# Layer 0 of a two-layer hybrid backbone: ten input-projection blocks by seven products of halves ahead of the attention, staggered mLSTM heads, half of the output projection beside them

## The chip, the core and the metric

The kernel runs on one core of a Trainium2 chip. A core has five engines with queues of their own: TensorE multiplies matrices (PE in the profile; PEld is its loading of weights), VectorE (DVE) works element by element, ScalarE (ACT) applies functions and copies, GpSimd (POOL) does small arithmetic and starts transfers, and SyncE (SP) starts transfers. Matmuls write to PSUM, eight banks of 128 x 512 float32; everything else lives in SBUF. The metric is the device time of one execution in microseconds. Three runs of the kernel before took 3549.83, 3545.3 and 3549.78 us; the median is 3549.78.

## What is computed

1024 latent tokens and 256 context tokens of width 1024 pass through two layers. Each layer normalizes, scales and shifts its input, projects it, mixes over tokens, and projects back with a gated residual. Layer 0 has two mixers side by side, one projection in and one out:

```python
qa, ka, va, za, qb, kb, vb, ob, zb, g = _split_cols(h @ w_in, AB_SIZES)   # nine blocks of 1024 columns, 16 gate columns
...
if rotary:
    qb, kb = _axial_rope(qb), _axial_rope(kb)
...
oa_l = _neighbourhood_attention(qa_l, ka_l, va_l, ka_c, va_c, rpb)        # 16 heads of 64
hb_l, hb_c = _mlstm_bidir(mb_l, mb_c, need_ctx)                           # 4 heads of 256, both directions
...
hb = jnp.swapaxes(hb, 1, 2).astype(ob.dtype) * jax.nn.sigmoid(_heads(ob, ML_HEADS))
hb = _rms(hb, h_norm.reshape(ML_HEADS, ML_DIM))
ya = oa.reshape(oa.shape[:2] + (NA_WIDTH,)) * jax.nn.silu(za)
yb = hb.reshape(hb.shape[:2] + (ML_WIDTH,)) * jax.nn.silu(zb)
return jnp.concatenate([ya, yb], axis=-1) @ w_out
```

Layer 1 has 16 recurrent heads (HGRN2) in the same frame. The change concerns layer 0; layer 1's code is touched where it shares helpers.

## The kernel before

All large projections are float32 in three matmuls: each operand is split into a rounded high part and a low rest (`split`, L71 on ScalarE, L72 on VectorE), and `dense` (L120 to L122) adds high x high, high x low and low x high over 8 depth tiles of 128. The normalized input h of a layer lies transposed in SBUF as `hh` and `hl`, ten tiles of 128 tokens wide. Weights come from memory in slabs of 128 x 512 (`wraw`), are split, and wait in a ring of six slabs (`wring`).

A *block* is 256 columns of the projection for all ten token tiles: 10 x 8 x 3 = 240 matmuls of 256 columns. `proj_out` makes one: it evicts pairs of tiles into `ev` (two buffers) and stores them with a POOL DMA (L275). There are 24 such blocks: four of attention values (`na_values`) and q, k, v, o, z of the four mLSTM heads (`ml_ahead`), stored in `md`.

Layer 0 runs in this order: modulation and norm; gates and the modulation rows of both layers, with blocks 0 to 2 of the attention values beside them; the attention, eight pairs of heads (`na_attn`) of ten tiles each, with the next pair's q, k (`na_qk`), z (`na_z`) and one block beside each; the mLSTM; the output projection. The last twelve blocks stand under `filler`, which gives them a late priority, so that the scheduler of the language places them in gaps of the mLSTM.

The mLSTM takes the heads one after another. `ml_load` fetches all ten chunks of a head, rotates q and k on VectorE (`rope`, L413 to L416), transposes them on TensorE and makes the scores; `ml_rec` then walks ten chunks in both directions. A chunk in one direction (a *unit* below) is five float32 matmuls of 258 columns: L451 into `acc`, two of L461 with the state `mC`, two of L470 whose result L478 adds to the state. `ml_out` gates and normalizes a finished chunk (L507 to L513, with an inverse root on POOL, L147) and transposes it (L517) for `yd`.

The output projection has two column halves (b = 1, 0) and two depth halves: q = 0 is the attention's part of `yd`, q = 1 the mLSTM's. `out_ahead` makes q = 0 of b = 1 into `oacc`, then `out_tile` q = 1 of it and, from a second weight array of 16 slabs, all of b = 0, with the next layer's norm and transposes (`mod_tr`) beside the last.

Layer 1's v and z projections use seven products of halves already (`q_sums`, `q_seven`): tokens, depth and columns are halved, and seven products of sums of the halves take the place of eight. `q_form` adds and splits weights, L872 to L874 multiply, `q_out` combines.

The order on each engine is not written by hand: the scheduler sets it from priorities, the buffers of each pool and its own estimate of time. DMA queues and engines work through their own lists in order.

## Time and profile before

| | |
|---|---|
| median of three runs | 3549.78 us |
| the profiled execution | 3547.46 us |
| its span, first to last instruction | 3545.7 us |
| mean granted clock of TensorE | 0.992 |
| PE busy, share of span, instructions | 3473.2 us, 98%, x24618 |
| DVE busy | 2311.4 us, 65%, x6182 |
| ACT busy | 1550.8 us, 44%, x3587 |
| POOL busy | 538.4 us, 15%, x880 |
| DMA | 347.19 MB, mean 98 GB/s |

A row of a group reads: line, engine, operation, output tile <- input tiles, sizes, count | busy time in us, mean of one in ns | idle time of the engine just before, and what ended it. Float32 matmuls appear as two passes each. Matmuls are pipelined: the duration of one is longer than the distance to the next, so a busy TensorE is not the same as one at its peak.

### The profile page before, as it was taken

To read this page: it belongs to the slowest core of one execution; us is meant where nothing else is said; L and a number is where in the kernel's file an instruction comes from. 1 tells how busy PE (TensorE), PEld (TensorE's weight loads), DVE (VectorE), ACT (ScalarE), POOL (GpSimd) and SP (SyncE) were. 2 spreads that over 40 slices of the span, in tenths; PEclk is the share of its full clock that TensorE was granted. 3 is DMA by queue.
4 is the path that set the end of the run, shared out by engine and by line. 5 is a ranking of instruction groups with operands and counts; after the bars stand their busy time and mean duration, and the time that the engine had idled before them with its cause. 6 is when DMAs were issued, how large, how long until landed. Compare 5 with 4: busy or idle time off the path is not lost.

```text
span 3545.7 us, 65436 instructions
## 1 busy us (share of the span) xinstructions
PE 3473.2 (98%) x24618; PEld 3175.5 (90%) x24618; DVE 2311.4 (65%) x6182; ACT 1550.8 (44%) x3587; POOL 538.4 (15%) x880
## 2 busy tenths in 40 slices
PE   8999999999999999998989999999999999999999
PEld 5879999999999999997778999989999999999877
DVE  4646666666754756655556866577777777777853
ACT  5545555455533433333345333344444444444431
POOL 2222222222211212211101222000100000000010
PEclk9999999999999999999999999999999999999999
DMA  5532323222234334324653322211211211211354
GB/s 210 173 105 74 83 70 83 75 82 83 76 99 153 109 106 144 101 89 137 199 160 125 102 102 102 81 37 55 64 44 54 60 55 48 60 60 46 111 174 126
DMA packets 361964, 347.19 MB, mean 98 GB/s; under 512 B 31064, under 2 KB 314904, under 8 KB 361520
## 3 DMA queue, kind: packets, MB, share of 16 engines
q1 hardware_dynamic: 323472, 242.61, 23.5%
q0 software_dynamic: 38176, 100.40, 8.2%
q8 instruction: 194, 3.18, 0.4%
q14 instruction: 122, 1.00, 0.1%
HBM read 266.66 MB, written 76.08 MB: 97 GB/s over the span
## 4 chain that ended last, share of the span: by engine, by line
PE 83%; issue 8%; DMA 4%; DVE 2%; POOL 1%; ACT 1%; SPq 0%; POOLq 0%; ACTq 0%; DVEq 0%
PE mm L122 14%; PE mm L120 14%; PE mm L121 14%; PE s L1041 6%; PE acc L677 2%; PE tr L657 2%; PE mm L731 2%; PE mm L732 2%; PE mm L733 2%; PE sa L873 2%; PE sa L872 2%; PE sa L874 2%; PE s L470 1%; PE acc L461 1%; PE s L1086 1%
## 5 line engine op out<-in xcount | busy, mean ns | idle before, releaser
L122 PE MATMUL mm<-wh,hl 128*128 128x256 f32 x2560 | 749.5, 293 | 0.3 <-DVE hl L253 0.3
L120 PE MATMUL mm<-wh,hh 128*128 128x256 f32 x2560 | 747.1, 292 | 0.0
L121 PE MATMUL mm<-wl,hh 128*128 128x256 f32 x2560 | 746.0, 291 | 0.0
L122 PEld LDWEIGHTS mm<-wh,hl 128*128 128x128 f32 x2560 | 489.1, 191 | 11.1 <-issue 4.1
L120 PEld LDWEIGHTS mm<-wh,hh 128*128 128x128 f32 x2560 | 489.3, 191 | 7.7 <-issue 1.5
L121 PEld LDWEIGHTS mm<-wl,hh 128*128 128x128 f32 x2560 | 489.3, 191 | 7.1 <-issue 0.5
L122 PE MATMUL mm<-hh,wl 128*128 128x512 f32 (+1 forms) x1344 | 490.9, 365 | 0.0
L120 PE MATMUL mm<-hh,wh 128*128 128x512 f32 (+1 forms) x1344 | 485.0, 361 | 0.0
L121 PE MATMUL mm<-hl,wh 128*128 128x512 f32 (+1 forms) x1344 | 483.7, 360 | 0.0
L121 PEld LDWEIGHTS mm<-hl,wh 128*128 128x128 f32 x1344 | 254.0, 189 | 32.1
L122 PEld LDWEIGHTS mm<-hh,wl 128*128 128x128 f32 x1344 | 253.9, 189 | 30.3
L120 PEld LDWEIGHTS mm<-hh,wh 128*128 128x128 f32 x1344 | 254.3, 189 | 29.2
L71 ACT CAST wh<-wraw 128x512 fp32r<-128x512 f32 x274 | 168.7, 620 | 209.1 <-PE mm L121 126.3
L1032 ACT COPY gksel<-gK 128x512 f32<-128x512 f32 x224 | 146.9, 662 | 213.7 <-PE s L1041 204.6
L731 PE MATMUL mm<-woh,yh 128*128 128x512 f32 x524 | 210.6, 403 | 16.3 <-issue 10.1
L72 DVE TENSOR_TENSOR wl<-wraw,wh 128x512 fp32r<-128x512 f32 x274 | 185.1, 685 | 56.6 <-ACT wh L71 54.5
L733 PE MATMUL mm<-woh,yl 128*128 128x512 f32 x524 | 209.5, 400 | 0.0
L732 PE MATMUL mm<-wol,yh 128*128 128x512 f32 x524 | 208.8, 399 | 0.0
L1041 PE MATMUL s<-gQ,gksel 128*128 128x128 f32 x1536 | 199.8, 276 | 0.0
L1041 PEld LDWEIGHTS s<-gQ,gksel 128*128 128x128 f32 x1536 | 192.4, 191 | 7.0
L145 POOL TENSOR_SCALAR gss<-gss 128x4 f32<-128x4 f32 x32 | 16.6, 518 | 968.0 <-ACT gjk L1111 968.0
L1062 DVE TENSOR_TENSOR gQ<-gQ,gT 128x256 f32<-128x256 f32 x384 | 143.1, 413 | 28.0 <-PE s L1041 28.0
(442 smaller groups left out, 7970.7 us busy)
## 6 DMA issues: line engine op xcount, KB each, us to landing
wraw<-yd SPq DMA_DIRECT2D x144, 256.0 KB
wraw<-in_wc_dram SPq DMA_DIRECT2D x128, 256.0 KB
wraw<-in_wab_dram SPq DMA_DIRECT2D x112, 256.0 KB
md<-ev POOLq DMA_DIRECT2D x100, 256.0 KB, 2.7
adar<-in_wada_dram POOLq DMA_DIRECT2D x32, 512.0 KB, 4.6
b<-in_wc_dram SPq DMA_DIRECT2D x64, 256.0 KB
vzd<-qo POOLq DMA_DIRECT2D x128, 128.0 KB, 2.2
adar<-in_wada_dram SPq DMA_DIRECT2D x16, 512.0 KB
```

The costliest lines, as they stand in the source:

```text
L71: nc.scalar.copy(hi, x)
L72: nc.vector.tensor_tensor(out=lo, in0=x, in1=hi.bitcast(F32), op=ALU.subtract)
L120: mm(ps, lhsT=lh(k), rhs=rh(k), start=(k == 0), stop=False)
L121: mm(ps, lhsT=lh(k), rhs=rl(k), start=False, stop=False)
L122: mm(ps, lhsT=ll(k), rhs=rh(k), start=False, stop=(k == nk - 1))
L657: nc.tensor.transpose(pt[:nk, i, :], pr[:, o : o + nk], self.ident)
L731: mm(ps, lhsT=yh[:, k, :], rhs=w.h(kk), start=(kk == 0), stop=False)
L732: mm(ps, lhsT=yh[:, k, :], rhs=w.l(kk), start=False, stop=False)
L733: mm(ps, lhsT=yl[:, k, :], rhs=w.h(kk), start=False, stop=(kk == 8 * len(qs) - 1))
L1032: nc.scalar.copy(ksel.rearrange("p (b s i) -> p b s i", s=2, i=h), pick(K))
L1041: nc.tensor.matmul(pa[:, c, :].rearrange("p (b s i) -> p b s i", s=2, i=h), lhsT=ksel[:, c * P : (c + 1) * P], rhs=qp[:, c * nbc : (c + 1) ...
L1062: nc.vector.tensor_tensor(out=t[:, i, :, s, :], in0=t[:, i, :, s, :], in1=bc(tot), op=ALU.mult)
```

## The change

Six things move, all in layer 0; the number of bytes computed is the same.

- **Seven products.** Ten blocks, in five sets of two column halves, are made by `q_two` and `q_seven` before the attention (`a_ahead`): attention values 2 and 3, and q and k of all four heads. Token tiles 0 to 4 and 5 to 9 are the row halves. A set is 7 x 5 x 12 = 420 matmuls instead of 480. The fourth operand of sums is built in place, over one quarter of `hh` and `hl`; that quarter is first copied to memory and copied back at the end (POOL DMAs). The first two products of the first two sets run early, while the sums are made; blocks v 1 and o 0 stand beside them. The rotation of q and k moves from `ml_load` to the result of each product, before the store.
- **The other blocks.** Attention values 0, 1 and v 0 stay in the first stage (with a ring of four slabs instead of six), z 0, o 1, z 1, v 2, o 2, z 2, v 3, o 3 stand beside the attention, z 3 beside the mLSTM.
- **Staggered heads.** `ml_all` starts a head every five steps, so that for most of the 25 steps two heads are under way, one in the first half of its chunks and one in the second. Chunks are loaded one step ahead. The scaling of v by the decay goes from VectorE to ScalarE, the factor 1/16 into the eviction of q, and two operations of `ml_out` become one.
- **Half of the output beside them.** `out_some` makes q = 0 of both column halves at steps 10 to 14 (into `oacc`) and 19 to 23 (stored to `x1`).
- **The rest of the output.** q = 1 of b = 1 follows, then q = 1 of b = 0, which loads its stored half sum; each has a ring of eight slabs.
- **Layer 1's seven products** work on pairs of token tiles (evictions of 512 columns) through the shared helpers.

Its core in the code:

```diff
-            with self.filler():
-                for h in range(4):
-                    for part in "vqk":
-                        if (part, h) not in self.md:
-                            self.ml_ahead(part, h)
-                for part in "oz":
-                    self.ml_ahead(part, 3)
...
+            with self.pp.phase(sa=4), tc.tile_pool(name="qa", bufs=1) as pool:
+                self.q_open([(0, 1), (1, 2), (3, 2)], a["wab"], (self.wp, "ev", 2), (self.wp, "wraw", 3), (pool, "qs", 2), 2)
+                self.a_ahead(pool)
...
+                self.ml_ahead("z", 0)
+                ahead = {2: ["o1"], 3: ["z1"], 4: ["v2"], 5: ["o2"], 6: ["z2"], 7: ["v3", "o3"]}
...
+                for g, at in self.ml_all(pool):
+                    with self.filler(), tc.issue_after(at.ins):
+                        if g in ML_AHEAD:
+                            self.ml_ahead(*ML_AHEAD[g])
...
+                        for b, g0 in ((1, ML_OUT[0]), (0, ML_OUT[1])):
+                            if g == g0:
+                                wq[b] = wo(0, b, [(yp, "wo", 8)] * 8)
+                            for tt in ML_ORDER[max(0, 2 * (g - g0)) : max(0, 2 * (g - g0) + 2)]:
+                                part(b, tt)
...
+    def a_ahead(self, pool):
...
+                nc.gpsimd.dma_start(out=self.a21[c, :, :, s], in_=a21[c][:, :, s])
+        S = {}
+        self.q_sums(pool, "2", S)
+        self.ml_ahead("v", 1, True)
+        self.ml_ahead("o", 0, True)
+        S["1"] = a21
+        self.q_sums(pool, "1", S)
+        todo = [("n", 2)] + [(p, h) for h in (0, 2) for p in "qk"]
...
+        us = [self.q_two(self.q_raw(pool, cols[i], ("11", "21")), S, sinks[i], pool) for i in range(2)] + [None] * 9
+        for i in range(len(todo)):
+            self.q_seven(self.q_raw(pool, cols[i]), S, sinks[i], pool, us[i])
+        for c in range(2):
+            nc.gpsimd.dma_start(out=a21[c], in_=self.a21[c])
...
+    def q_seven(self, raw, S, sink, pool, u=None):
+        tt = self.nc.vector.tensor_tensor
+        u = u or self.q_two(raw, S, sink, pool)
+        v, m5 = {}, {}
+        for i, ps in self.q_product("s1", S, self.q_form(raw, "11", "12")):
             m5[i] = ps
...
+        for g in range(5 * 3 + NT):
+            for h in range(4):
+                scores = load(h, g + 1 - 5 * h) if 0 <= g + 1 - 5 * h < NT else []
+                if 0 <= g - 5 * h < NT:
+                    at = self.ml_rec(h, g - 5 * h, seqs, st[h], pool)
+                for score in scores:
+                    score()
+            yield g, at
```

What the scheduler makes of it shows in the order on the engines. First TensorE in the recurrence. Before, a stretch of head 0: L451, L461 and L470 are the unit's matmuls, the rows with `mm` a block's.

```order
L451 MATMUL acc_18400<-mv_17625,mSD_18398 128x258
L120 MATMUL mm_14932<-wh_14701,hh_121 128x256
L470 MATMUL s_18364<-mvw_18362,mkn_17747 128x258
L121 MATMUL mm_14932<-wl_14700,hh_121 128x256
L122 MATMUL mm_14932<-wh_14701,hl_122 128x256
L120 MATMUL mm_14932<-wh_14701,hh_121 128x256
L121 MATMUL mm_14932<-wl_14700,hh_121 128x256
L470 MATMUL s_18366<-mvw_18362,mkn_17747 128x258
```

Now, in the stretch before the output's first half (L462, L472, L479 are the same three matmuls; L394, L400 and L526 are transposes of q, k and an output):

```order
L462 MATMUL acc_18854<-mv_3221_18519,mSD_18852 128x258
L526 MATMUL tr_18712<-ident_73,mhs_3261_18622 128x128
L479 MATMUL s_18737<-mvw_18733,mkn_3184_18425 128x258
L526 MATMUL tr_18712<-ident_73,mhs_3261_18622 128x128
L479 MATMUL s_18819<-mvw_18817,mkn_3232_18548 128x258
L479 MATMUL s_18821<-mvw_18817,mkn_3232_18548 128x258
L472 MATMUL acc_18809<-mC_18640,mqc_18813 128x258 x2
L526 MATMUL tr_18757<-ident_73,mhs_3250_18594 128x128
L394 MATMUL tr_18773<-ident_73,mqn_18771 128x128 x2
L472 MATMUL acc_18854<-mC_18665,mqc_18858 128x258 x2
```

The block's matmuls between the units are gone there, and units of two heads stand between each other; of the 80 units 36 lie in two such stretches.

Second, VectorE and the rotation. Before, it stands among the units (L464 scales v):

```order
L464 TENSOR_SCALAR mvw_17900<-mv_17835,mD_17892 128x258
L413 TENSOR_TENSOR mkn_17712<-mld_17713,mrope_17553 128x256
L414 TENSOR_TENSOR mrs_17715<-mld_17713,mrope_17553 128x256
L464 TENSOR_SCALAR mvw_17925<-mv_17858,mD_17917 128x258
L413 TENSOR_TENSOR mqn_17734<-mld_17735,mrope_17553 128x256
```

Now it stands among the seven products' own work: L75 splits a weight slab, L932 and L956 combine results, L1002 to L1005 rotate.

```order
L956 TENSOR_TENSOR qu_501_3031<-qu_501_3031,sa_3776 128x512
L1004 TENSOR_TENSOR ev_3767<-ev_3767,qs_3769 128x2x64
L1005 TENSOR_TENSOR ev_3767<-ev_3767,qs_3769 128x2x64
L1002 TENSOR_TENSOR qs_3803<-ev_3801,mrope_2089 128x512
L1003 TENSOR_TENSOR ev_3801<-ev_3801,mrope_2089 128x512
L75 TENSOR_TENSOR wl_3931<-b_578_3585,wh_3932 128x512
L1004 TENSOR_TENSOR ev_3801<-ev_3801,qs_3803 128x4x64
L1005 TENSOR_TENSOR ev_3801<-ev_3801,qs_3803 128x4x64
L75 TENSOR_TENSOR wl_3935<-b_579_3587,wh_3936 128x512
```

The rotation has moved in front of weight splits that TensorE's next product needs.

Third, POOL in front of the attention. `ar` is the inverse root that the first transposes (`na_qk`, L548 before) wait for, `avw` are values of the attention. Before:

```order
L157 DMA adar_1495<-in_wada_dram 128x2x512
L700 DMA avw_2592<-vd_64 96x1x128 x4
L700 DMA avw_2741<-vd_64 128x1x128 x4
L145 TENSOR_SCALAR ar_2174<-ar_2174 128x8
L145 TENSOR_SCALAR ar_2249<-ar_2249 128x8
L147 TENSOR_TENSOR ar_2174<-ar_2174,mhalf_77 128x8
```

Now (L1029 brings back the saved quarter of `hh` and `hl`, L963 stores results of the seven products):

```order
L963 DMA md_72<-ev_5390 128x256
L1029 DMA hh_123<-a_8_70 128x4x640
L1029 DMA hl_124<-a_8_70 128x4x640
L963 DMA md_72<-ev_5423 128x2x256
L963 DMA md_72<-ev_5456 128x2x256
```

And, six stores further on:

```order
L963 DMA md_72<-ev_5827 128x256
L963 DMA md_72<-ev_5860 128x2x256
L963 DMA md_72<-ev_5893 128x2x256
L152 TENSOR_SCALAR ar_6001<-ar_6001 128x8
L154 TENSOR_TENSOR ar_6001<-ar_6001,mhalf_78 128x8
```

The first pair's value loads are gone from POOL (they stand on SP); the copy back and the last stores stand in their place. On TensorE four of the five pairs of the first projection stood ahead of those transposes; now three do, behind the seven products.

More of the change, by code (lines that the diff above doesn't have):

```diff
@@ L500, in ml_out @@
+        return at
     def ml_out(self, h, tt, hs, pool):
@@ new lines, in q_plain @@
+    def q_plain(self, raw, early, sink, pool):
+        for c in range(2):
+            ps = []
+            w = early if not c else self.q_form(raw, "12")
+            for r, i in [(r, i) for r in (1, 0) for i in range(self.half)]:
+                ps.append((r, i, self.q_ps(1)))
+                self.q_nat(ps[-1][2], self.q_quarter(f"{r + 1}1"), i, w, last=False)
+            w = self.q_form(raw, "22" if c else "21")
+            for r, i, p in ps:
+                self.q_nat(p, self.q_quarter(f"{r + 1}2"), i, w, first=False)
+                o = self.t(self.qo[0], [P, 512], F32, *self.qo[1:])[:, 0:256]
+                self.nc.scalar.copy(o, p)
+                sink(c, r * self.half + i, 1, o)
@@ new lines, in q_product, with q_keep, q_out @@
+    def q_product(self, n, S, w):
+        a = S[n[1]] if n[0] == "s" else self.q_quarter(n)
+        for u in self.units:
+            ps = self.q_ps(u[1])
+            for j in range(u[1]):
+                self.q_nat(ps[:, j * 256 : (j + 1) * 256], a, u[0] + j, w)
+            yield u, ps
+    def q_keep(self, pool, tag, m):
+        return self.t(pool, [P, m * 256], F32, f"{tag}{m}", self.qn * sum(x[1] == m for x in self.units))
+    def q_out(self, sink, r, c, u, in0, in1, op):
+        o = self.t(self.qo[0], [P, 512], F32, *self.qo[1:])[:, 0 : u[1] * 256]
+        self.nc.vector.tensor_tensor(out=o, in0=in0, in1=in1, op=op)
+        sink(c, r * self.half + u[0], u[1], o)
@@ L1258, in build @@
+                w2 = wo(1, 1, [(yp, "wo", 8)] * 8)
+                self.gate_bc(0, yp, 2, 1)
+                for tt in [8, 9, 3, 4, 2, 5, 1, 6, 0, 7]:
+                    xt = self.t(yp, [P, 512], F32, "ox", 2)
+                    self.out_tile(w2, 1, tt, self.yd, self.xin(tt), xt, yp, yp, 2, part=acc[:, tt, :])
+                    nc.gpsimd.dma_start(out=self.x1[tt * P : (tt + 1) * P, 512:D], in_=xt)
             l0.close()
```

569 lines of the change are left out of this document (291 added, 278 removed).

## The prediction

> **What bounds the kernel now.** I read the page first: where the busy time lies, and which engine carries the chain that ended last.
>
> ```profile
> PE 3473.2 (98%) x24618; PEld 3175.5 (90%) x24618; DVE 2311.4 (65%) x6182; ACT 1550.8 (44%) x3587; POOL 538.4 (15%) x880
> PE 83%; issue 8%; DMA 4%; DVE 2%; POOL 1%; ACT 1%; SPq 0%; POOLq 0%; ACTq 0%; DVEq 0%
> ```
>
> TensorE is the bound: 98% busy and 83% of the chain. So a matmul less is time less, as long as what feeds it keeps up. Next I cut the span by stage (columns: stretch, length, busy time of PE, PEld, DVE, ACT, POOL with instruction counts, granted clock, DMA share, GB/s).
>
> ```profile
> 218.00:250.00 32.00, 23.70 (x136) 20.83 (x135) 14.84 (x26) 11.80 (x24) 12.71 (x16) 0.89 0.22 61
> 250.00:1100.00 850.00, 849.64 (x7356) 808.14 (x7355) 548.43 (x1746) 427.11 (x1152) 187.55 (x246) 1.00 0.29 80
> 1100.00:1289.00 189.00, 183.70 (x1379) 176.95 (x1378) 110.57 (x367) 71.19 (x194) 32.16 (x93) 0.99 0.47 142
> 1289.00:1364.00 75.00, 75.00 (x485) 69.72 (x484) 55.56 (x198) 32.02 (x88) 16.81 (x46) 1.00 0.32 94
> 1364.00:1600.00 236.00, 233.92 (x1747) 225.14 (x1746) 137.16 (x461) 87.12 (x234) 41.98 (x86) 1.00 0.35 109
> 1600.00:1700.00 100.00, 90.33 (x500) 78.56 (x500) 54.57 (x153) 38.07 (x96) 18.83 (x33) 0.93 0.43 135
> 1700.00:1800.00 100.00, 87.69 (x368) 71.07 (x367) 53.98 (x87) 33.84 (x59) 6.89 (x12) 0.91 0.69 211
> 1800.00:1920.00 120.00, 119.56 (x602) 100.75 (x601) 72.58 (x182) 64.94 (x173) 13.58 (x28) 1.00 0.41 124
> 1920.00:2000.00 80.00, 76.61 (x631) 75.41 (x630) 67.79 (x125) 33.27 (x65) 14.05 (x26) 1.00 0.37 121
> 2000.00:2200.00 200.00, 200.00 (x1684) 200.00 (x1683) 138.27 (x297) 65.19 (x131) 44.15 (x82) 1.00 0.31 108
> ```
>
> The attention (250 to 1100) and layer 1's products (2000 to 2200) leave TensorE no gap. It waits in front of the attention (218 to 250) and from the end of the mLSTM into the output projection (1600 to 1800). In both the clock sinks too. Its longest waits, by the view of waits (us in total, times, longest), lie there:
>
> ```profile
> PE mm L731 <- issue: 10.1, 1, 10.1
> PE tq L548 <- issue: 8.3, 1, 8.3
> PE tr L517 <- DVE mhs L513: 8.0, 1, 8.0
> PE tr L517 <- ACT myt L518: 5.1, 3, 2.5
> PE mm L731 <- DVE oacc L759: 2.2, 1, 2.2
> ```
>
> **The change part by part.** The sum is made against the profiled execution's own time, 3547.46 us (span 3545.7), which is 2.3 us (0.07%) under the median of the runs, 3549.78.
>
> *Seven products for eight.* Ten blocks of 10 token tiles x 8 depth tiles x 3 matmuls are 2400 matmuls of 256 columns; seven eighths are 2100, so 300 go. Between 2000 and 2200 nothing but such matmuls runs: 200 us / 1684 = 0.119 us each; at 0.12, **-36 us**. Nothing hides a matmul on the bound engine, so this end is firm.
>
> *The stall in front of the attention.* POOL's list in time order (start, us, what) shows what TensorE waited for:
>
> ```profile
> 221.73 3.34 POOL L700 DMA_DIRECT2D avw<-vd  x5 [18.81 <-issue]
> 225.48 2.02 POOL L700 DMA_DIRECT2D avw<-vd  x3 [0.42 <-issue]
> ```
>
> Eight loads of values, 5.4 us, start when the attention's buffers open and stand ahead of the inverse root that the first transposes need; four of the projection's five pairs are done by then, so nothing covers. Now the first pair's loads go by SP, and three pairs (144 matmuls, 17 us) follow the seven products ahead of those transposes. What stands before the root is the last stores of the seven products, one of 0.7 us after the last result; 17 us cover that and the root's chain. So 8.3 us of idle and 11% of 32 us of clock (3.5 us) go: **-11**. Late instead could be the restored quarter of h (2.6 MB by POOL's queue): its first reader is the third pair, 11.5 us in. At the 142 to 211 GB/s of the rows above the copy takes 12 to 18 us, but it is queued four products (4 x 7.2 us) ahead. The stores behind it hold both staging buffers meanwhile, and the smaller weight ring has its first matmul nearer to a split: 0 to 10, I take **+3**.
>
> *From the mLSTM to the output.* 12.3 + 9.7 us of idle in the two stretches from 1600, and a clock 7 and 9% low, of which part falls on the idle time itself; I count 11 of those 16. Four heads one after another leave the last one's tail without cover; now half of the output (480 matmuls of 512 columns) runs beside the recurrence, the other half's first weights are split in the same ring, and the late two slabs of the old first half are gone: **-33**. New in its place: the first slabs of the second ring wait for the last tile of the first half (**+2**, bounds 0 and 8).
>
> *The seven products' own feeders.* A set of 420 matmuls is 50 us. VectorE's share, by these rows:
>
> ```profile
> L72 DVE TENSOR_TENSOR wl<-b,wh 128x512 fp32r<-128x512 f32 x70 | 46.4, 685 | 28.1 <-ACT wh L71 27.9
> L862 DVE TENSOR_TENSOR b<-b,b 128x512 f32<-128x512 f32 x43 | 28.6, 683 | 0.2
> L884 DVE TENSOR_TENSOR qo<-qu,sa 128x256 f32<-128x256 f32 x24 | 10.0, 418 | 13.0 <-PE sa L874 13.0
> L414 DVE TENSOR_TENSOR mrs<-mld,mrope 128x256 f32<-128x256 f32 x64 | 26.9, 420 | 3.0 <-DMA mld<-md 2.4
> L415 DVE TENSOR_TENSOR mqn<-mqn,mrs 128x128 f32<-128x128 f32 x32 | 9.3, 290 | 0.7
> ```
>
> 14 splits 9.6, 10 sums of weights 6.8, 21 sums of results (7 narrow at 0.418, 14 wide at 0.685) 12.5, and on the q and k sets the rotation of 16 tiles (singles 1.42, pairs 2.2, ten units) 19: 48 of durations. In layer 1 a set of 39.9 us has 31.4 by these rows and shows 69% busy, so durations overlap to 0.88 of their sum: some 42 busy here, 85% of 50 us. Layer 1's sets run without a gap. The halves' sums in front are 85 operations of 0.68, 58 us, beside v and o (58 us) and the early products (29 us); layer 1's sums cost 3.4 us of idle (1920 to 2000). I take one such bill for the front and one for the four tight sets: **+8**, bounds 0 and 30.
>
> *The staggered recurrence.* Here the cover gets thin. Eleven of its twelve filler blocks leave the stage; z of head 3 and the 480 output matmuls remain. One unit is a head's chunk in one direction. The chain of waits prices its matmuls (start, us, what):
>
> ```profile
> 1454.72 0.87 PE acc L461 x4
> 1479.39 0.87 PE acc L461 x4
> 1811.69 0.88 PE tr L229 x8
> ```
>
> Four passes take 0.87, and a unit needs five matmuls of two passes: 2.17 us. By the order on TensorE 36 of the 80 units, in two stretches, have no filler: 167 such matmuls, 100 transposes (0.11 each) and 32 scores, together 90 us or 2.5 a unit. VectorE's lines for a unit:
>
> ```profile
> L478 DVE SCALAR_TENSOR_TENSOR mC<-mC,mcw,s 128x258 f32<-128x258 f32 x128 | 61.3, 479 | 31.8 <-PE s L470 30.6
> L457 DVE TENSOR_TENSOR mqc<-mqT,mcw 128x256 f32<-128x256 f32 x72 | 30.0, 422 | 36.0 <-ACT mqT L386 26.2 <-ACT mcw L454 9.6
> L443 DVE TENSOR_TENSOR mE<-mmask,mGb 128x128 f32<-128x128 f32 x80 | 22.6, 282 | 7.7 <-DMA mGb<-Gd 4.4 <-ACT mD L445 3.2
> L484 DVE TENSOR_SCALAR msm<-acc,thr 128x1 f32<-128x1 f32 x80 | 16.9, 211 | 1.8 <-PE acc L461 1.6
> L488 DVE TENSOR_TENSOR msm<-acc,msm 128x1 f32<-128x1 f32 x80 | 12.1, 151 | 0.8
> L489 DVE RECIPROCAL msm<-msm 128x1 f32<-128x1 f32 x80 | 12.8, 160 | 1.5
> L494 DVE SCALAR_TENSOR_TENSOR mhs<-acc,msm,mhs 128x256 f32<-128x256 f32 x40 | 19.1, 479 | 0.4
> L507 DVE SCALAR_TENSOR_TENSOR mhs<-mlo,mhs 128x256 f32<-128x256 f32 x40 | 16.8, 420 | 1.8 <-DMA mlo<-md 1.4
> ```
>
> Two state updates 0.958, the scaled query 0.422, exponent and scores 2 x 0.282, the three small ones 0.522, half of a sum 0.240 and half of an output's two (2 x 0.420): 3.13 us. Durations overlap, to 0.88 of their sum as above. So VectorE needs at least 2.75, more than TensorE's 2.5, and now sets these stretches; in one with a recurrence (1289 to 1364) it got to 74%, which would be 3.7. The old units between the two chain rows above (seven such groups, six intervals, 24.67 us) took 4.1, with filler between them. I take 3.1, nearer to the work than to the old pace, since two heads offer independent work: 36 x 0.6 = +22 (bounds +9 at 2.75 and +57 at 4.1), +5 for the first chain, minus the 5.3 + 2.1 us of idle of the stretches from 1100 and 1364 that are replaced: **+20**. The scaling of v moves to ScalarE and 1/16 into an eviction, the rotary work leaves the stage; both are in the unit's sum.
>
> *The attention.* It loses one of nine fillers, and in two places (end of pair 1, end of pair 6) some 170 matmuls stand without any, about six tiles. VectorE's largest lines of a tile (80 tiles in all):
>
> ```profile
> L611 DVE TENSOR_REDUCE ast<-s 128x1 f32<-128x256 f32 x160 | 66.7, 419 | 26.0 <-PE s L610 23.8
> L622 DVE CUSTOM_DVE_ANT_0 aP<-s,aP 128x288 f32<-128x288 f32 (+3 forms) x128 | 62.2, 486 | 6.5 <-DMA aP<-in_nab_dram 3.7 <-PE s L621 0.8
> L667 DVE COPY apT<-tr 128x256 f32<-128x256 f32 (+3 forms) x224 | 88.6, 417 | 27.9 <-PE tr L657 24.8 <-PE acc L677 0.9
> ```
>
> VectorE needs two maxima, two score sums and 2.8 copies a tile, 3 us by these rows alone, an estimated 4.5 with the small ones: 27 us for six. TensorE's part is an estimated 17 (170 at 0.1). 27 less 17, with some overlap: **+8**, bounds 0 and 20.
>
> *The last quarter of the output.* A tile has 24 output matmuls instead of 48 beside the same normalization: 1800 to 1920 shows ACT at 54% with them all; with half of them gone it comes close to TensorE's pace. **+4**, bounds 0 and 15. Layer 1 from there on keeps its matmuls; wider evictions there save nothing, TensorE covers them already.
>
> Sum: 3547.5 - 36 - 11 - 33 + 3 + 2 + 20 + 8 + 8 + 4 = **3512**; on the runs' level, 2 us higher, **3514** (-1.0%). This case reaches from 3490 to 3537.
>
> At nothing I cost the DMAs that come with it: two more stores a set on POOL (15% busy), ten copies of the quarter out, ten stores and ten loads of half sums, and a second load of two sets' first weights on SP's queue. The transfers of the attention and product stages fill 0.29 to 0.31 of the DMA engines. Were that cover gone, it would be the copy back that is late, priced above, or loads of the last quarter, which are in its bounds.
>
> **The rivals.** *All is covered.* If the scheduler's order leaves the thin stretches no more idle than the old stage had, the additions shrink to about 10: 3478, on the runs' level 3480. For it speaks that 250 to 1100 and 2000 to 2200 show none; against it that VectorE's work a unit is above TensorE's.
>
> *Slower: the recurrence's pace.* If an unfilled unit takes T, that term is 36 x (T - 2.5) - 2; the rest comes to 3494 on the runs' level. No change is reached at T = 4.1, the old pace, and slower by 0.2% from 4.3. VectorE's and ScalarE's queues run in order, so one late eviction would hold both heads; the old rows had 4.1 with one head, though filled. At 4.4: 3560.
>
> *The saving does not arrive.* If every product of the five sets waits 1 us for its weights behind rotations on VectorE (35 boundaries), 35 us come back: 3547, on the runs' level 3549.
>
> *The clock.* Stretches with short matmuls between transposes could count as idle:
>
> ```profile
> 1100.00:1157.00 57.00, 54.77 (x458) 53.91 (x457) 25.05 (x79) 18.67 (x49) 6.35 (x30) 1.00 0.61 188
> 1234.00:1289.00 55.00, 51.93 (x425) 51.41 (x424) 27.30 (x86) 19.13 (x53) 9.46 (x15) 0.97 0.49 153
> ```
>
> At half clock a unit's matmuls need 5.0 instead of 2.5, against a pace of 3.1: 36 x 1.9 = 68 us more, 3582. The rows speak against it: with 2.2 us of idle scattered over 57 us, transposes among them, the clock stayed full, and with 3.1 us in 55 it lost 3%. [...]
>
> **How the numbers follow.** Likeliest case 0.50 (3514); all covered 0.19 (3480); slow recurrence 0.13 (around 3560); saving lost 0.12 (around 3549); clock 0.06 (3582). 0.2%, about 7 us, is what a measurement of this kernel can tell from no change; so faster ends at 3542.7 and slower begins at 3556.9. Faster: the first two and a third of the fourth with a little of the third, 0.75. Same: most of the rest of the fourth and some of the third, 0.10. Slower: 0.15. The range leaves out the clock, the upper third of the slow recurrence and a tail below: 3470 to 3560.
>
> **What would show it.** Right: no gap above 3 us before the first transposes of the attention; TensorE 95% busy or more in the seven-product stage, whose DVE share is 80 to 90%; in the mLSTM's two unfilled stretches TensorE at 75 to 85% with DVE above it, 112 us for the 36 units; no clock below 0.95 in the output stage. Wrong: idle TensorE waiting for weight splits between products, unfilled units above 4 us, or waits for POOL's queue, where the copies of the saved quarter stand between stores.

## The result, and the profile after

| | before | after |
|---|---|---|
| median, and range, of the runs (us) | 3547.43 (3545.3 to 3549.83) | 3557.49 (3551.63 to 3562.33) |
| profiled execution, its span | 3547.46, 3545.7 | 3552.23, 3550.4 |

The ratio is 1.0026, 95% interval 1.0017 to 1.0035: a little slower, by about 10 us, where 36 us less were forecast (3514 against the 3549.78 of the first three runs). In a second series the changed kernel took 3553.8 against 3547.2 us, ratio 1.0015 (1.0005 to 1.0024). The 300 matmuls did go, and something gave their time back. The page of the changed kernel, its busy times and its chain:

```profile
PE 3466.5 (98%) x24318; PEld 3140.5 (88%) x24318; DVE 2406.6 (68%) x6079; ACT 1596.0 (45%) x3690; POOL 529.2 (15%) x840
PE 84%; issue 5%; DMA 4%; DVE 3%; ACT 2%; POOL 1%; SPq 0%; POOLq 0%; ACTq 0%; DVEq 0%
```

24618 - 24318 is 300, yet TensorE is busy only 6.7 us less, not 36. Busy time counts a matmul that stands alone with its whole duration, and one in a dense row only with its distance to the next (0.275 and 0.109 us for a transpose), so thinner rows and a lower clock raise it (a score matmul of 256 columns lasted 0.38 us at 1294.6, at full clock, and 0.58 at 1300.6, at half clock); new idle time comes on top. The view of waits between 218 and 2242 names whom TensorE waits for (us in total, times, longest):

```profile
PE tr L394 <- ACT mqT L396: 6.9, 3, 4.8
PE s L619 <- DVE ast L634: 5.6, 8, 0.9
PE tr L526 <- ACT myt L527: 4.7, 3, 3.8
PE tr L394 <- DMA mqn<-md: 3.4, 2, 1.7
PE mm L743 <- ACT yh L74: 2.5, 1, 2.5
```

The two long waits of before (10.1 in front of the output, 8.3 in front of the attention) are gone; shorter ones on the recurrence (`mqT`, `myt`) and on the attention's maxima (`ast`) have come. By stage (stretch, length, busy PE, PEld, DVE, ACT, POOL, clock, DMA share, GB/s), first after, then before; the stages are front of the attention, attention, mLSTM, output:

```profile
218.00:588.00 370.00, 367.36 (x3008) 363.06 (x3007) 283.18 (x526) 99.33 (x179) 61.40 (x84) 1.00 0.34 103
588.00:1380.00 792.00, 779.56 (x6660) 731.03 (x6661) 524.39 (x1707) 401.55 (x1106) 172.82 (x222) 0.99 0.28 77
1380.00:1776.00 396.00, 371.04 (x1957) 309.28 (x1955) 248.37 (x802) 226.18 (x638) 78.25 (x216) 0.99 0.49 149
1776.00:2000.00 224.00, 214.71 (x1289) 190.09 (x1288) 166.49 (x321) 121.95 (x307) 32.13 (x62) 0.98 0.55 177
```

```profile
218.00:279.00 61.00, 52.70 (x379) 49.83 (x378) 28.85 (x53) 24.98 (x53) 18.57 (x22) 0.94 0.15 41
279.00:1098.00 819.00, 818.64 (x7097) 777.14 (x7096) 533.97 (x1718) 413.92 (x1124) 180.40 (x238) 1.00 0.29 82
1098.00:1704.00 606.00, 588.94 (x4139) 555.66 (x4139) 358.62 (x1181) 229.37 (x614) 111.06 (x259) 0.99 0.40 122
1704.00:2000.00 296.00, 279.86 (x1577) 243.95 (x1576) 194.04 (x393) 131.07 (x295) 34.52 (x66) 0.97 0.49 153
```

To see idle time and lengthened matmuls in one number, I price every matmul at the distance to the next that its shape has in the gap-free stretches of before (0.12 us for 256 columns, 0.227 for 512, 0.217 for a pass of 258, 0.109 for a transpose, 0.088 for the attention's narrow ones), and call *lost* what a stage takes beyond that sum (us; stages cut at their first and last matmul):

| stage | before: length, work, lost | after: length, work, lost | lost more |
|---|---|---|---|
| first stage, to 218 | 218.0, 183.6, 34.4 | 218.0, 181.1, 36.9 | +2.5 |
| in front of the attention | 60.6, 49.8, 10.8 | 370.3, 363.4, 6.9 | -3.9 |
| attention | 819.1, 818.7, 0.4 | 792.1, 766.8, 25.3 | +24.9 |
| mLSTM | 605.9, 578.7, 27.2 | 395.0, 348.8, 46.1 | +18.9 |
| output, layer 1's products | 577.6, 553.2, 24.5 | 505.7, 488.0, 17.7 | -6.8 |
| layer 1's recurrence and output | 1258.5, 1224.4, 34.1 | 1263.1, 1224.4, 38.7 | +4.6 |

Work falls by 36 us, as forecast; lost time rises by 40. In the profiled executions layer 1's recurrence starts at 2281 in both: layer 0 came out even. The loss sits where TensorE has no filler, that is, no independent matmuls to do while a chain waits (its *cover*; a tile or unit without it is called *bare* below). The next rows are the stretches without it: the tiles around the end of pair 1, those around the end of pair 6, and two in the recurrence.

```profile
776.00:802.00 26.00, 20.55 (x154) 16.27 (x154) 20.20 (x75) 13.90 (x42) 5.94 (x8) 0.82 0.23 73
1286.00:1316.00 30.00, 23.00 (x181) 18.24 (x180) 18.48 (x79) 11.43 (x40) 6.01 (x9) 0.89 0.35 100
1459.00:1533.00 74.00, 61.28 (x295) 47.43 (x295) 58.46 (x203) 50.81 (x152) 19.60 (x51) 0.95 0.65 203
1643.00:1697.00 54.00, 51.04 (x250) 39.24 (x249) 44.88 (x167) 37.66 (x119) 14.05 (x38) 1.00 0.42 129
```

In the attention 7 tiles stand bare and take 46.8 us, 6.6 each, with 3.3 of matmuls in them: 23 us lost. In the recurrence 52 units stand in gaps of over 4 us between filler (165 us in all): 3.17 each, 2.38 of it matmuls: 41 lost. Of the 52, 42 stand in the two long stretches and 10 in four gaps of 6 to 9 us between lumps of filler.

### The profile page after: what moved, and what is told of

Its sections match the earlier page's. It is cut to its first block, busy times and chain, and to the rows that moved or that the text cites. A ratio compares the mean times of both kernels' runs of the same rounds, so it can differ in the third digit from the quotient of the medians.

```text
span 3550.4 us, 64785 instructions
## 1 busy us (share of the span) xinstructions
PE 3466.5 (98%) x24318; PEld 3140.5 (88%) x24318; DVE 2406.6 (68%) x6079; ACT 1596.0 (45%) x3690; POOL 529.2 (15%) x840
## 4 chain that ended last, share of the span: by engine, by line
PE 84%; issue 5%; DMA 4%; DVE 3%; ACT 2%; POOL 1%; SPq 0%; POOLq 0%; ACTq 0%; DVEq 0%
PE mm L129 14%; PE mm L128 14%; PE mm L127 14%; PE s L1129 6%; PE sa L128 3%; PE sa L127 3%; PE sa L129 3%; PE acc L689 2%; PE mm L743 2%; PE mm L745 2%; PE mm L744 2%; PE tr L669 2%; PE s L1174 1%; PE tr L129 1%; PE tr L128 1%
## 5 line engine op out<-in xcount | busy, mean ns | idle before, releaser
L127 PE MATMUL mm<-wh,hh 128*128 128x256 f32 x1980 | 567.0, 287 | 1.2 <-ACT wh L74 1.1
L128 PE MATMUL mm<-wl,hh 128*128 128x256 f32 x1980 | 567.7, 287 | 0.3 <-DVE wl L75 0.2
L129 PE MATMUL mm<-wh,hl 128*128 128x256 f32 x1980 | 565.6, 286 | 0.0
L127 PEld LDWEIGHTS mm<-wh,hh 128*128 128x128 f32 x1980 | 378.2, 191 | 8.3 <-issue 4.0
L128 PEld LDWEIGHTS mm<-wl,hh 128*128 128x128 f32 x1980 | 378.8, 191 | 4.2 <-DVE wl L75 0.7
L129 PEld LDWEIGHTS mm<-wh,hl 128*128 128x128 f32 x1980 | 378.3, 191 | 3.6 <-issue 1.2
L743 PE MATMUL mm<-woh,yh 128*128 128x512 f32 x544 | 223.0, 410 | 8.3 <-ACT woh L74 4.4
L745 PE MATMUL mm<-woh,yl 128*128 128x512 f32 x544 | 220.0, 405 | 0.2 <-DVE yl L75 0.2
L744 PE MATMUL mm<-wol,yh 128*128 128x512 f32 x544 | 220.2, 405 | 0.0
L75 DVE TENSOR_TENSOR wl<-wraw,wh 128x512 fp32r<-128x512 f32 x272 | 184.4, 687 | 43.7 <-ACT wh L74 38.1
L74 ACT CAST wh<-b 128x512 fp32r<-128x512 f32 x136 | 84.5, 622 | 209.2 <-PE sa L129 96.2
```

The source lines that it names most:

```text
L74: nc.scalar.copy(hi, x)
L75: nc.vector.tensor_tensor(out=lo, in0=x, in1=hi.bitcast(F32), op=ALU.subtract)
L127: mm(ps, lhsT=lh(k), rhs=rh(k), start=(first and k == 0), stop=False)
L128: mm(ps, lhsT=lh(k), rhs=rl(k), start=False, stop=False)
L129: mm(ps, lhsT=ll(k), rhs=rh(k), start=False, stop=(last and k == nk - 1))
L743: mm(ps, lhsT=yh[:, k, :], rhs=w.h(kk), start=(kk == 0), stop=False)
```

## The experiments

"The changed kernel" below is 3557.5 in its first series and 3553.8 in its second, 3554.2 over both. These two series of one and the same kernel differ by 3.7 us, so a difference of that size between two versions says little.

**What a longer execution loses.** The changed kernel once more.

> The changed kernel once more, for its spread and for a second profile. Its eleven runs lie between 3551.6 and 3562.3 us, the profiled one near the bottom. Theory: the spread comes from the stretches where TensorE is thin (1288 to 1310 and 780 to 803 in the attention, 1459 to 1533 and 1643 to 1697 in the recurrence), so a slower run shows a lower granted clock there: median 3557 again, and a profile above 3555 has at least 3 us more in these stretches. Rival: the spread sits in the last 250 us, where the profile of the changed kernel is already 5 us behind the one of before; then these stretches are equal to within 1 us.

Median 3553.8 (3547.3 to 3557.2); the profiled execution took 3554.16, 2 us more than the first. The median missed the forecast by 3 us, and no profile above 3555 came. The second one lost 2.7 us more in the attention and 1.7 more in the mLSTM, and 2 less in layer 1, as the theory has it for these two. Of the first eleven executions the longest, 3562.3, has a mean granted clock of 0.987, and the two below 3552 have 0.991 and 0.992. Cut into 4 us, the bare place between pairs 6 and 7 shows how (first profile, then second):

```profile
1294.00:1298.00 4.00, 2.20 (x13) 1.34 (x11) 3.03 (x14) 2.02 (x8) 0.58 (x1) 0.96 0.33 99
1298.00:1302.00 4.00, 3.17 (x14) 2.48 (x16) 2.12 (x11) 1.92 (x8) 0.00 (x0) 0.50 0.52 176
1302.00:1306.00 4.00, 3.27 (x28) 2.69 (x24) 1.80 (x8) 0.37 (x1) 0.00 (x0) 0.68 0.02 2
1306.00:1310.00 4.00, 3.03 (x28) 2.20 (x30) 2.41 (x10) 2.59 (x9) 0.00 (x0) 1.00 0.32 88
```

```profile
1298.00:1302.00 4.00, 2.59 (x18) 2.03 (x19) 2.24 (x11) 1.45 (x5) 0.00 (x0) 0.73 0.38 132
1302.00:1306.00 4.00, 3.44 (x22) 2.75 (x20) 1.66 (x6) 0.46 (x2) 0.00 (x0) 0.50 0.05 8
1306.00:1310.00 4.00, 3.32 (x12) 2.28 (x12) 2.00 (x9) 2.02 (x8) 0.00 (x0) 0.50 0.28 82
1310.00:1314.00 4.00, 4.00 (x28) 3.33 (x27) 1.66 (x7) 0.71 (x4) 1.24 (x2) 0.56 0.00 0
```

By the trace's record of the clock TensorE ran at half clock for 6.8 us in one execution and 13.7 in the other, in the same place. In the whole attention it was 17 and 27 us: 10 us more for the 2.7 us more that were lost.

**Do the seven products arrive?** The five sets by eight plain products each.

```diff
-        for i in range(len(todo)):
-            self.q_seven(self.q_raw(pool, cols[i]), S, sinks[i], pool, us[i])
+            for c in range(2):
+                w = [self.q_form(raw, f"{k}{c + 1}") for k in (1, 2)]
...
+                                self.q_nat(ps[...], self.q_quarter(f"{r + 1}{k + 1}"), u[0] + j, w[k], k == 0, k == 1)
```

> The five sets of two blocks ahead of the attention by plain products of halves: eight quarter products a set, no sums of halves, no sums of weights or results. Everything behind is the changed kernel. Theory (the seven products arrive whole): 300 matmuls of 256 columns more at 0.12 us, 36 us, less the 7 us of idle that stand between 218 and 300 under the sums: 29 us slower than the changed kernel (22 to 36). Rival (the saving is eaten by the sums and their waits): within 6 us.

3590.3 against 3553.8 beside it: +36.5 us, just above the range. In front of the attention 398 us of matmuls instead of 363, and 6.3 lost instead of 6.9. So the products bring all they save; VectorE's sums cost TensorE under 1 us there. The rival falls.

**The loads in front of the attention.**

```diff
-                (nc.gpsimd if p2 else nc.sync).dma_start(out=vw[: 4 * W, j, :], ...)
+                nc.gpsimd.dma_start(out=vw[: 4 * W, j, :], ...)
```

> One part undone: the eight loads of values of the first pair go by the queue of POOL again, ahead of the inverse root of the first query and key. Theory (those loads made the stall in front of the attention): a wait of 8 us before the first transposes of the attention and a clock below 0.95 there, 8 to 11 us slower than the changed kernel. Rival (the three pairs of projection that follow the seven products, 17 us, cover the 5.4 us of loads wherever they are queued): within 3 us.

3558.8 (3549.2 to 3559.1): 4.6 us above the changed kernel's 3554.2, 1.3 above its first series. That is nearer to the rival, and the profile decides for it: the front loses 7.3 us instead of 6.9, at a clock of 0.99 and 1.00. No wait of TensorE for the first transposes shows up between 218 and 700; the longest is the same as in the changed kernel (2.0 there):

```profile
PE tr L127 <- ACT hh L74: 2.1, 1, 2.1
```

The loads did stand ahead of the root again: on POOL from 526.4 to 531.7, the root behind them 5 us later than in the changed kernel, the first transposes 5.8 us later, with 5.5 us more of matmuls done by then. So the 8.3 us stall of before went through the three pairs of projection that now stand behind the seven products, not through the queue of the loads.

**Is it the place of the cover in the attention?** One block a pair, and each chunk behind a tile of its own.

```diff
+                    n = 5 * len(ahead.get(p2, [])) + 8 * (p2 < 7)
+                    self.slots = [self.at[i * NT // n] for i in range(n)]
...
+            with self.slot():
+                for j in range(2):
+                    self.proj_nat(ps[:, j, :], w, tt + j, 0, 256)
```

> The same filler blocks in the attention, one for each of pairs 1 to 7, and each chunk of a block, of the next pair's query and key and of its gate queued on TensorE behind a tile of its own, so that they spread over the pair's ten tiles. Theory (the place of the cover, not its amount, costs the 24 us that TensorE stands idle or at a low clock at the end of pairs 1 and 6): 18 us faster than the changed kernel (12 to 24), no stretch of 10 us without filler, at most 5 us of idle in the attention. Rival (VectorE or the latency of a tile's chain needs all of the filler; spread out, the idle is the same): within 4 us of the changed kernel.

3574.4 against 3553.8: 20.6 us slower. The theory falls, and the rival was too mild: the attention lost 36.7 us. Here pair 0 had filler throughout, but only 21 to 36 matmuls of it in 10 us, where the changed kernel has 54 (first this kernel, then the changed one under full filler):

```profile
618.00:680.00 62.00, 53.44 (x396) 45.61 (x396) 43.42 (x142) 33.71 (x93) 9.05 (x12) 0.92 0.23 60
```

```profile
640.00:702.00 62.00, 62.00 (x516) 57.57 (x515) 42.80 (x137) 32.52 (x87) 11.84 (x17) 1.00 0.23 64
```

VectorE has the same work per us in both. A tile took 9 us under thin filler (7 tiles in the 62 us), not much less than under full filler (6.5 tiles), and only 6.6 when it stands bare. That the order on TensorE's queue, made for the slower pace, is what holds the tile is argued, not shown; the rows show that thin filler has the price of both. Besides, all but 5 matmuls of the block o of head 3 were done before the attention ended, where the changed kernel leaves 112 of them to cover the step into the recurrence, and the mLSTM lost 12 us more. So the 20.6 us are two losses, and only the 11 us of the attention speak of thin filler.

**Is it the amount?** One set back to plain blocks, beside the attention.

```diff
-        todo = [("n", 2)] + [(p, h) for h in (0, 2) for p in "qk"]
+        todo = [(p, h) for h in (0, 2) for p in "qk"]
...
-ahead = {2: ["o1"], 3: ["z1"], 4: ["v2"], 5: ["o2"], 6: ["z2"], 7: ["v3", "o3"]}
+ahead = {1: ["n2"], 2: ["o1"], 3: ["z1"], 4: ["n3"], 5: ["v2"], 6: ["o2", "z2"], 7: ["v3", "o3"]}
```

> The set of the two blocks of values goes back from the seven products to plain blocks beside the attention: blocks 2 and 3 of the values behind pairs 1 and 4, and the others moved so that every pair from 1 on has at least one block. Four sets of products are left. Theory (TensorE lacks cover in the attention by amount, and 480 matmuls of cover are worth more there than the 60 that a set saves): 60 matmuls more, 7 us, and 23 of the attention's 25 us of idle and low clock gone: 16 us faster than the changed kernel (10 to 22). Rival (the attention's idle does not depend on its cover): 7 us slower.

3572.2: 18 us slower, so as a forecast of the time the theory missed. In the attention it was right half way: 57 us of matmuls more took 47, and 15.1 us were lost instead of 25.3. But the front lost 26.3 instead of 6.9. The mLSTM lost some 6 us more as well. The values had been the set without rotation; now the rotated sets follow the sums of the halves at once:

```profile
280.00:360.00 80.00, 66.17 (x496) 62.57 (x495) 66.84 (x127) 16.16 (x27) 8.62 (x13) 0.96 0.25 75
```

```profile
PE sa L127 <- DVE qu L956: 4.2, 1, 4.2
PE sa L127 <- DVE ev L932: 2.5, 1, 2.5
```

In the same 80 us of the changed kernel TensorE is busy 77.6 us and VectorE 67.5, as much as here; 11 us of its operations are rotation there, 21 here. That the order of the sets is what costs the 19 us in front is argued from these figures, not shown by a run of its own.

**Is it the place in the recurrence?**

```diff
-ML_AHEAD = {0: ("z", 3)}
+ML_Z = (0, 2, 4, 6, 8)
+ML_N = [2] + [1] * 8
...
+                        if g in ML_Z:
+                            pair(2 * ML_Z.index(g))
```

> In the mLSTM the five chunks of the block z of head 3 are queued at steps 0, 2, 4, 6, 8 instead of all at step 0, and the first ten output tiles at two in step 10 and one in each of steps 11 to 18 instead of two in each of steps 10 to 14. Same instructions. Theory (a unit of the recurrence needs 3.2 us however much TensorE work lies beside it, so 0.7 us of filler a unit hides it): of the 46 us that TensorE loses between 1385 and 1776, 30 go (18 to 36). Rival (the order on the queues of VectorE and ScalarE sets the pace, whatever lies on TensorE): less than 8 us faster.

3547.6 (3542.3 to 3554.6), 6.2 us faster than the changed kernel beside it: inside the rival's bound. Where the theory had 30 of the mLSTM's 46 us go, about 4 went. Bare units went from 3.17 to 2.94 us, but there were 58 of them instead of 52.

**Do late weights hold up the recurrence?** In the changed kernel ScalarE waits for a load of output weights with the recurrence's evictions behind it (start, us, what):

```profile
1633.41 0.38 PE L394 MATMUL tr<-ident,mqn 128*128 128x128 f32 x2
1633.62 0.38 PE L400 MATMUL tr<-ident,mkn 128*128 128x128 f32 x2
...
1636.38 0.62 ACT L74 CAST woh<-woraw 128x512 fp32r<-128x512 f32 x1 [4.52 <-DMA woraw<-in_woab_dram]
...
1638.42 0.39 ACT L396 ACTIVATE mqT<-tr 128x256 f32<-128x256 f32 x1
...
1638.86 0.56 PE L394 MATMUL tr<-ident,mqn 128*128 128x128 f32 x2 [4.85 <-ACT mqT L396]
```

```diff
-                            raws = [yp, 4, "woraw"]
+                            raws = [yp, 8, "woraw"]
...
+                            if g == (9 if b else 18):
+                                with tc.issue_after(acts[g - 1]):
+                                    for x in cuts:
+                                        self.split(*x)
```

> The weights of the two output blocks beside the recurrence are loaded into eight staging buffers instead of four, and their splits are queued on ScalarE behind step 8 (first block) and step 17 (second) instead of wherever the order put them, so that no cast stands on ScalarE's queue ahead of its load. Same instructions. Theory (at 1470 and 1635 of the changed kernel ScalarE waits 2.8 and 4.5 us for such a load, with the recurrence's evictions behind it, and TensorE stands 4 to 5 us each time, at a lower clock after it): 9 us faster (5 to 13), no wait of ScalarE above 1.5 us for the output weights. Rival (the units' pace is set by their own chain, and the casts only fill a hole): within 3 us.

3555.0 (3546.9 to 3562.1), no faster. ScalarE's wait for the weights fell from 19.3 us (longest 8.1) to 3.0 (longest 1.5), but the cast of the attention's rows for the same output now stood ahead of its load:

```profile
ACT yh L74 <- DMA wraw<-yd: 4.3, 1, 4.3
PE s L482 <- ACT mST L412: 3.8, 1, 3.8
```

A bare unit took 3.20 us. What the staging did save, 5 us, showed behind the mLSTM, in the stage of the output (12.7 lost instead of 17.7).

**All three at once.** Values, spread and staging together.

> Values back as plain blocks in the attention, the recurrence's filler spread over the steps, and the output weights staged ahead, all three together. Theory (three separate losses): 16 + 7 + 9 = 32 us faster than the changed kernel, 25 under the kernel before (18 to 35). Rival (they are one loss, since what is covered in one place comes back in the next): less than 15 us faster than the changed kernel.

3556.7, no gain: 18 us more lost in front (25.0) and 7 us of matmuls more stood against 10 less lost in the attention (15.4), 5 in the mLSTM (41.5) and 7 in the output (10.2). The sum of theories failed with its largest term.

**Spread and staging.** The two edits without the values; run in two series.

> The recurrence's filler spread over the steps and the output weights staged ahead, both together, blocks of the attention as in the changed kernel. Theory (two losses, in two places: 4 to 7 us within the recurrence by the spread, 5 to 7 behind it by the staging, which showed between the last output of the heads and layer 1): 12 us faster than the changed kernel (8 to 17). Rival (what the staging saves comes back as slower units): 6 us, as the spread alone.

> The version with spread filler and staged output weights once more, beside the next one. Theory: 3540 us again, 0.2% under the kernel before. Rival (its first series was a lucky one, as the version with the earlier chunks came out 6 us higher with less waiting): 3546, no difference from the kernel before.

3539.9 (3536.5 to 3542.6) and 3540.5 (3533.8 to 3550.3): about 14 us under the changed kernel, and the ratio to the kernel before is 0.9982 both times (0.9972 to 0.9991, 0.9974 to 0.9991). The theory of two places holds: the mLSTM loses 39.1 instead of 46.1, the output stage 10.9 instead of 17.7. This is the fastest version, by a little.

**All of the cover dealt out anew.** z of head 3 beside pair 1, one output tile a step.

```diff
-                ahead = {2: ["o1"], ...
+                ahead = {1: ["z3"], 2: ["o1"], ...
-ML_OUT = (10, 19)
+ML_OUT = (3, 14)
```

> The block z of head 3 moves from the recurrence to the end of pair 1 of the attention, so that every pair from 1 on has a block; in the recurrence the twenty output tiles stand one in each of steps 3 to 12 and 14 to 23, with eight staging buffers and the splits queued on ScalarE behind steps 1 and 12. Same instructions as the changed kernel. Theory (the cover counts by how it is dealt out over the bare places: attention 25 us to 13, recurrence with the step into the output 53 to 40): 25 us faster than the changed kernel (12 to 35), 17 under the kernel before. Rival (each stage keeps its loss, as the last experiments had it come back): less than 8 us faster.

3542.6 (3537.1 to 3547.8), ratio 0.9988 (0.9979 to 0.9996): 12 us under the changed kernel, at the low end of the theory. The attention took one block more (28 us of matmuls) in 20.7 us and lost 18.1; the recurrence, that block poorer, lost 51.0.

**Is VectorE the limit of a unit?**

```diff
-            nc.vector.tensor_tensor(out=E, in0=self.mask[:, d, :], in1=Gb, op=ALU.subtract)
...
-            nc.scalar.activation(Dm, E, AF.Exp, bias=...)
+            nc.scalar.activation(Dm, Gb, AF.Exp, scale=-1.0, bias=...)
```

> The subtraction of the running sum from the mask (0.28 us of VectorE a unit) is left out of the recurrence, ScalarE's exponential reads the running sum itself, with scale -1; so the causal mask is missing. Theory (VectorE's work sets the pace of a bare unit): 40 bare units at 2.9 instead of 3.2 us, 11 us faster than the changed kernel (8 to 14). Rival (VectorE, 75% busy there, is not what a unit waits for; the order between three engines is): less than 4 us.

3549.8 (3547.1 to 3559.8): 4 us faster. A bare unit took 3.12 instead of 3.17 to 3.20 us where 0.28 us of VectorE were gone. The difference is hardly larger than that between the two series of the changed kernel, and nearer to the rival's bound of 4 than to the theory's 8 to 14: VectorE's work alone does not set the pace.

**Loads out of the way.** First the weights opened earlier, then every cast of the filler behind the recurrence.

```diff
-ML_Z = (0, 2, 4, 6, 8)
+ML_Z = (0, 1, 2, 4, 6)
-                        if g == 9:
+                        if g == 7:
...
+                    late = tc.issue_after(acts[g - 1]) if g >= 7 else nullcontext()
+                    with self.filler(), late, tc.issue_after(at.ins):
```

> As the version with spread filler and staged output weights, and the chunks of z of head 3 at steps 0, 1, 2, 4, 6, so that the normalized rows are given back at step 7 and the first output weights are loaded there, with their splits behind step 9. Theory (in that version ScalarE still waits 3.7 us at 1516 for the first load, because the staging opens only after the last chunk, and TensorE stands 4.8 us): this wait and 5 us of idle go, 4 us under that version (2 to 7), 20 under the changed kernel. Rival (steps 7 to 9 are bare instead, and their units take back what the wait gave): within 2 us of that version.

3546.7 (3542.0 to 3550.8), ratio 0.9998: the wait for the weights went (2.7 us in all, longest 1.0), but the time is 6 to 7 us above the version it starts from. In the profiles the mLSTM lost the same in both, within 1 us. The attention lost 2.6 us more and layer 1 some 5 more, on the same instructions, with 10 and 7 us more at half clock (mean granted clock 0.990 against 0.991); why this version met more of it was not tried.

> As the version with the chunks of z at steps 0, 1, 2, 4, 6, and from step 7 on every operation of the filler on ScalarE, the casts of the attention's rows too, is queued behind the recurrence of the step before. When only the weights' casts were held back, a wait of 4.3 us showed up at the cast of the rows instead. Theory (a cast that is queued ahead of its load holds up the recurrence, whichever load it is): no wait of ScalarE above 2 us for the weights or the rows, 8 us less lost in the recurrence than in the changed kernel, 3 us under the version that is run beside it. Rival (bare units take 3.2 us whatever waits are taken from ScalarE): not faster than the version beside it.

3545.3 (3541.5 to 3550.3), 5 us above the version beside it: the rival. Waits of 2.5 us for rows and 0.9 for weights were the longest left, and TensorE waited for other things instead:

```profile
PE acc L481 <- DVE mhs L522: 4.9, 3, 2.6
PE tr L413 <- DMA mqn<-md: 3.5, 2, 1.9
PE s L426 <- ACT mkT L421: 2.8, 3, 2.1
```

A bare unit takes 2.9 to 3.2 us in every one of these kernels. Its matmuls need 2.4; in the bare stretch from 1459 ScalarE and VectorE work 2.4 and 2.7 us a unit (50.81 and 58.46 us for 21.5 units), no single wait that was taken away shortened it, and only spreading the filler did (2.94). What holds a bare unit so far above its matmuls stays open.

## Why the prediction was wrong, point by point

The matmuls of the sum were right. It failed at two of its smaller terms, what TensorE loses without cover in the attention and in the recurrence, and together they ate the gain; two other figures came out right by luck.

- **-36, seven products**: held. 36 us of work gone; undoing it cost 36.5.
- **+8, the products' feeders**, and **-11, +3, in front of the attention**: sum 0 forecast, -1.4 measured (rows one and two of the table). The sum is right by luck: the run with plain products, which has no sums and 137 us of VectorE's work in front instead of 283, lost 6.3 there against 6.9, so the feeders cost under 1 us and not 8, and the other two terms brought some 2 us and not 8. The stall itself went, by the three pairs of cover; the change of queue had no part in it. Of the rival that the saving does not arrive, nothing was seen in the changed kernel, but without the set of values 19 us more were lost in front.
- **+8, the attention**: the first step that failed; 24.9 measured. It took a bare tile at an estimated 4.5 us against 2.8 of matmuls, from VectorE's busy time. A bare tile took 6.6 against 3.3: a tile is a chain through three engines, and VectorE was 78% busy in the first bare place and 62% in the second, not full. The low clock (0.82 and 0.89) was left out too; at 17 us of half clock in the attention it can make up at most 8.5 of the 24.9.
- **+20, the recurrence**: the second. The count was wrong: 36 units were read from the order as standing without filler, but 52 stood so on the chip. The two stretches hold 42, and 10 more stand between lumps of filler, which comes a whole tile of matmuls at a time. 52 x 0.79 is 41 where 22 stood in the sum. The pace came out (3.1 forecast, 3.17 measured), but not for the reason given, that VectorE sets it: VectorE was busy 79 and 83% of the two stretches, under TensorE's 83 and 95%, where the prediction had it above, and 0.28 us less of its work a unit gave 0.05. So the 3.1 was luck.
- **-33, +2, end of the mLSTM, and +4, last quarter of the output**: together with the recurrence -7 forecast, +12.1 measured (rows four and five). The recurrence's count alone is 19 of this, so these terms were, by subtraction, right within a few us. That the output's weights stand on ScalarE ahead of their loads was not in the sum; 5 to 7 us of the stage behind go to it, since the staging took them out.
- **Layer 1, at nothing**: 4.6 us more in the first profile, 2.5 in the second. Its recurrence has the same 7332 matmuls in both. From 2300 on the trace has 22 us at half clock after and 13 before (15 in the second profile), and in the profiles of the fourteen experiments this stretch, the same in all of them, loses from 1 to 6 us more than before. So it is scatter of the clock in part; that all of them lie above the one profile of before leaves 1 us or more open.
- **The clock, a rival at 0.06**: happened in part. Not in the recurrence, where it was placed (0.95 and 1.00), but in the attention's bare tiles (0.82 and 0.89), and longer executions of the changed kernel show a lower clock (0.987 at 3562.3 us, 0.991 at 3551.6). No run shows that short matmuls between transposes count as idle for the clock: the bare stretch at 1643, with 44 transposes among its 250 matmuls, kept 1.00.

The forecast of 3512 and the profiled 3552 differ by 40 us: 17 in the attention, 19 in the mLSTM and the output, 4.6 in layer 1, less 1.4 in front.

## What to carry to other kernels

Independent matmuls beside a chain are cover, and moving them ahead has a price: a block given back to the attention here took 21 us for its 28 us of matmuls, so a quarter of what moves away stays behind as idle time, and it must be taken from the saving. Price a bare step by the length of its chain through all engines as it runs without filler, not by the busy time of one engine, and count bare steps between lumps of filler too. How to deal out short cover has no one answer here: spread thinly over the attention's tiles it cost 11 us more there than in one piece with the rest bare, while in the recurrence the spread over the steps brought 4 us.

## What the runs showed of the hardware

TensorE's granted clock went to 0.50 at a place where it never waited longer than 0.8 us at a time (1294 to 1306; in the second profile 1.4 us), though a fifth to nearly a half of each 4 us was idle in small pieces; of the 178 matmuls that start from 1286 to 1316, 42 are transposes and 76 products with 64 columns of weights (128*64, 96*64 and 72*64 in their rows). After the single wait of 3.8 us at 1470 it went to 0.50 too:

```profile
1470.00:1474.00 4.00, 0.63 (x3) 0.22 (x2) 2.13 (x6) 2.78 (x7) 0.13 (x2) 1.00 1.07 349
1474.00:1478.00 4.00, 3.19 (x9) 1.92 (x9) 3.83 (x9) 4.00 (x14) 1.70 (x4) 0.65 1.03 320
1478.00:1482.00 4.00, 3.27 (x10) 2.40 (x10) 3.44 (x10) 2.89 (x8) 1.26 (x2) 0.50 0.81 278
```

In the four bare stretches above TensorE was idle for 21, 23, 17 and 5% of the time, and the mean granted clock was 0.82, 0.89, 0.95 and 1.00. The second profile of the same kernel has 0.74 and 0.77 in the first two, with 21.11 and 22.94 us busy where the first has 20.55 and 23.00. So the busy time of a stretch alone does not give its clock; what does was not shown.
